# Scores of gated linear attention as half-width products copied under masks, one product for selected keys and values, and compressed values padded to 128 rows

## The chip, the cores and the metric

The kernel runs on one core of a Trainium2 chip. The metric is the device time of one execution in microseconds (us), the median of the runs. The core's engines work beside each other and wait for one another through semaphores: TensorE (PE: products and transposes; PEld is its loading of the stationary operand), VectorE (DVE), ScalarE (ACT), GpSimd (POOL) and SyncE (SP, which only starts the transfers here).

## The reference

One decoder layer over 256 positions of width 2048. One projection of the normalised input feeds two mixers: four heads of gated linear attention (GLA) and eight query heads of sparse attention (NSA) with two key and value heads. Their outputs go through one output projection, and a gated feed-forward layer follows. All of it is in float32. Cut to the parts that the change touches:

```python
def gla_mixer(q, k, v, gate_lr, out_gate, gate_w2, gate_b, norm_g):
    ...
    qc = chunks(q.astype(jnp.float32) * GLA_DK ** -0.5, GLA_DK)
    ...
    def step(state, inp):
        qi, ki, vi, gi = inp
        b = jnp.cumsum(gi, axis=2)
        o_inter = jnp.einsum('bhtd,bhde->bhte', qi * jnp.exp(b), state)
        decay = jnp.exp(jnp.where(causal, b[:, :, :, None, :] - b[:, :, None, :, :], -jnp.inf))
        scores = jnp.einsum('bhtd,bhsd,bhtsd->bhts', qi, ki, decay)
        o_intra = jnp.einsum('bhts,bhse->bhte', scores, vi)
        ...
    o = rms_norm(o, norm_g) * jax.nn.silu(out_gate.astype(jnp.float32)).reshape(b_, s, h, GLA_DV)

def nsa_mixer(...):
    ...
    v_cmp = compress(heads(vc_raw, hk), v_pos, v_w1, v_w2)      # 15 compressed blocks
    ...
        sc = jnp.einsum('bhgqd,bhnd->bhgqn', qb, k_cmp).astype(jnp.float32) * scale
        mc = cmp_end[None, :] <= t[:, None]
        pc = jax.nn.softmax(jnp.where(mc, sc, NEG), axis=-1) * mc
        o_cmp = jnp.einsum('bhgqn,bhnd->bhgqd', pc.astype(v_cmp.dtype), v_cmp)
    ...
```

## The kernel before

**Stages.** The input projection runs over column groups of `w_in`, 512 wide, in the order that the last lines of the kernel give (L1062 to L1068): first the low-rank gate with half of the output gate, then the other half, then q, k and v of GLA, then the raw keys and values of NSA (`C_KC` compressed, `C_KS` selected, `C_KW` window), then its queries. The output projection follows in two halves (`w_out_half`), and then the feed-forward layer, which takes most of the program. Each weight is loaded in float32 and split into two parts (`split`, L129 on ScalarE and L130 on VectorE), and every product of a float32 matrix is made as three products of the parts (`chunk`, L261: high by high, high by low, low by high). Such a product of 512 columns is one instruction. Products that aren't split (the scores of GLA, L513) are plain float32, which TensorE runs as two passes, so each of them shows up twice in the trace.

**Work beside the projections.** Everything small is written as generators that are put on two lists, `urgent` and `later`. `drive` takes one step of them for every few steps of a projection. A scheduler then fixes the order on each engine; engines take their own list in order. So the mixers run between the products of the projections, and the engines' lists decide who waits for whom.

**GLA.** Inside a chunk the decay between two positions is built from levels: `LEVELS` is 0 (the diagonal) and the block lengths 1 to 64. `gla_decay` makes, per pair of heads, one array `e[l]` per level, in which every second block of length l holds decayed queries and the others decayed keys (L484 to L495). `gla_scores` is run for 4 heads and 2 blocks of 128 positions, 8 times in all. For each level it multiplies `e[l]` with itself (L513), 128 by 128, four levels to a bank of PSUM; L515 multiplies the four with their masks `lmask` into a scratch array `m`, and after both banks L518 adds the eight levels up. The masks hold ISQ (the scale of the queries) where a level counts and 0 elsewhere. `gla_out` (L525 to L535) multiplies the scores with the values, `gla_turn` turns the result for the output projection.

**NSA.** `ev_kv(0)` empties the banks of the selected keys and values, `ev_kv(1)` those of the window's. `compress` makes 15 compressed keys and values for each head; the values lie in `vcm`, 15 rows. `nsa_scores` computes the probabilities, `c` being those of the 15 compressed blocks; `nsa_out` turns them (L193, through `turn`) and multiplies them with the values (L817), first with `vcm`.

**Buffers.** PSUM has eight banks of 128 by 512 (`bank()`), which projections and side work share. SBUF slots come from rings: `g4` (24), `g2` (13), `g1` (7), `small` (12).

The lines that decide how often L261 runs for selected keys and values, where `parts` gives each column group its own bank:

```python
for i, (a, m) in enumerate(((xh, wh), (xh, wl), (xl, wh))):
    for (off, w), bk in zip(parts, banks):
        last["mm"] = mm(bk[t], a[:, k, t * P:(t + 1) * P], m[:, off:off + w], ...)
...
proj(C_KS, ev_kv(0), ((0, 256), (256, 256)))
```

Of the kernel before, what the change touches and what calls it, by code (L numbers as in the profile page):

```python
# [9 lines left out]
F32R = mybir.dt.float32r  # L10
# [26 lines left out]
def kernel(  # L37
# [37 lines left out]
    def f32(t):  # L75
        return t.bitcast(F32)
# [131 lines left out]
    def cols_rest():  # L208
        for _ in range(8):
            yield  # L210
        with behind(last["dma"]):
            small_loads()
        for _ in range(20):
            yield
        pc = bank()
        transpose(pc[:, 0:P], rows2)
        transpose(pc[:, P:P + 20], rows[:20, :], 20)
        nc.vector.tensor_copy(cols[:, 36:164], pc[:, 0:P])
        nc.vector.tensor_copy(cols[:, 16:36], pc[:, P:P + 20])
        TS(kgain, gains[:, 1:4], gains[:, 0:1], None, ALU.mult)  # L220

# [128 lines left out]
    def constants():  # L350

        nc.gpsimd.memset(lmask, ISQ)
        for li, l in enumerate(LEVELS):
            if l == 0:
                affine(lmask[:, li, :], [[-1, P]], 0, 1)
                affine(lmask[:, li, :], [[1, P]], 0, -1)
                continue
            nb = P // (2 * l)
            v = lmask[:, li, :].rearrange("p (b h i) -> p b h i", h=2, i=l)
            nc.gpsimd.memset(v[:, :, 0, :], 0.0)  # L360
            affine(v[:, :, 1, :], [[-2 * l, nb], [0, l]], 0, 1)
            affine(v[:, :, 1, :], [[2 * l, nb], [0, l]], l - 1, -1)

        cnegf = g1([2, P])
        nc.gpsimd.memset(cnegf, 0.0)
        affine(cnegf, [[0, 2], [-1, P]], 0, 1, NEG)
        nc.vector.tensor_copy(cneg, cnegf)
        nc.vector.tensor_copy(identb, ident)

        nc.gpsimd.memset(mneg, 0.0)  # L370
        affine(mneg, [[P, NT], [-16, NCMP]], -31, 1, NEG)
        nc.gpsimd.memset(mone, 1.0)
        affine(mone, [[P, NT], [-16, NCMP]], -31, 1, 0.0)
# [131 lines left out]
    def gla_scores(h, b, res):  # L505
        tb = slice(b * P, (b + 1) * P)
        m, e = g4([NLEV, P]), dec[h // 2]
        for half in range(2):
            p = bank()
            for j in range(4):  # L510
                l = LEVELS[4 * half + j]
                u, w = (e[l][:, h % 2, tb],) * 2 if l else (kT[:, h, tb], qT[:, h, tb])
                mm(p[:, j * P:(j + 1) * P], u, w, start=True, stop=True)  # L513
                yield
            TT(m[:, 4 * half:4 * half + 4, :], p.rearrange("p (l t) -> p l t", l=4),  # L515
               lmask[:, 4 * half:4 * half + 4, :], ALU.mult)
        sc = g1([P])
        nc.vector.tensor_reduce(sc, m.rearrange("p l t -> p t l"), AX.X, ALU.add)  # L518
        res["s"] = sc

    def gla_out(h, r0, r1):
# [6 lines left out]
        act(sof, pof[:, 0:P], AF.Copy, scale=ISQ)  # L528
# [13 lines left out]
        TS(ro, ss, 1.0 / 256, EPS, ALU.mult, ALU.add)  # L542
# [61 lines left out]
    def ev_kv(br):  # L604
        def f(banks):
# [5 lines left out]
            for t in range(NT):  # L611
                pv = banks[1][t][:, :S]
# [42 lines left out]
    vcm = [cp.tile([NCMP, 2, P], F32R, name=f"vcm{i}") for i in range(2)]  # L655
    N2 = 2 * NCMP

    def compress():

        uT = st["uT"]  # L660
        for w, w1 in enumerate((k_w1, v_w1)):
# [44 lines left out]
            else:  # L706
                for h in range(2):
                    mm(pk[:NCMP, h * P:(h + 1) * P], hid[:, h * NCMP:(h + 1) * NCMP], cw2[:, 1, :], start=True, stop=True)
                in_parts(vcm[0], vcm[1], pk[:NCMP, :S].rearrange("p (h d) -> p h d", h=2))
# [35 lines left out]
    def nsa_scores(kv, t, res):  # L745
# [25 lines left out]
        c = small([4, NCMP])  # L771
# [18 lines left out]
        res.update(pr=pr, c=c)  # L790

    def nsa_out(kv, t, res):
# [6 lines left out]
        def turn(i):  # L799
            pt = bank()  # L800
            n = P if i else NCMP
            for j in range(4):
                src = pr[j][:, todo[i][0], todo[i][1] * P:(todo[i][1] + 1) * P] if i else c[:, j, :]
                transpose(pt[:n, j * P:(j + 1) * P], src)
                if j % 2:
                    yield
            pts.append((g2([512], F32R)[:n], g2([512], F32R)[:n]))
            in_parts(*pts[i], pt[:n, :])
# [256 lines left out]
    drive([proj(C_KC, ev_kc), proj(C_KS, ev_kv(0), ((0, 256), (256, 256))),  # L1065
# [45 lines left out]
```

## Time and profile before

| what | value |
|---|---|
| time, median of 3 runs | 1139.52 us (1139.39 to 1140.56) |
| span of the profiled execution | 1138.1 us, that is 1.4 us under the median of the runs |
| TensorE busy | 1125.4 us, 99% of the span |
| VectorE busy | 926.0 us, 81% |
| ScalarE busy | 604.7 us, 53% |
| GpSimd busy | 23.5 us, 2% |
| granted TensorE clock | 1.00 throughout |
| transfers | 213.44 MB, 188 GB/s on average |

How to read it: a page shows one profiled execution. The groups give line, engine, operation, output and input with their shapes, the number of instructions, busy time and the mean duration of one in ns, and behind the bar how long the engine had been idle just before them and what ended that. Matmuls are pipelined: an instruction lasts longer than the distance to the next one, so TensorE's pace is read from the distance between starts, or from the length of a stretch divided by the number of its products. A span of the chain or of the timeline begins with its start in us and its length in us.

### The profile page before, as it was taken

The numbers are of one execution on the slowest core, as the hardware profiler recorded it, in microseconds if no ns is written. First come the engines' busy times: TensorE is split into PE (matmuls) and PEld (weight loads), VectorE is DVE, ScalarE is ACT, GpSimd is POOL, SyncE is SP. The second block draws the span as 40 slices with busy tenths as digits, with TensorE's granted clock in tenths as the row PEclk, the third lists the DMA queues.
The fourth block names the chain that finished last, engine by engine and source line by source line (L and its number), as shares of the span: only waits on it lengthen the run. The fifth ranks groups of instructions, "written<-read, shape, count | busy, mean of one in ns | idle before, by whom it ended". The sixth has DMA issues, their size and how long they took to land.

```text
span 1138.1 us, 14334 instructions
## 1 busy us (share of the span) xinstructions
PE 1125.4 (99%) x5545; PEld 932.0 (82%) x5545; DVE 926.0 (81%) x1150; ACT 604.7 (53%) x742; POOL 23.5 (2%) x53
## 2 busy tenths in 40 slices
PE   9999999999999999999999999999999999999998
PEld 8888889998777787788888888888888888888886
DVE  6547779987479578999898897979798897979793
ACT  7654466544476486564555555364555455454540
POOL 3000000100000000000000000000000000000000
PEclk9999999999999999999999999999999999999999
DMA  7655543445843354665666566565665665665652
GB/s 273 226 185 185 185 148 113 154 149 165 301 163 112 116 180 150 209 235 192 213 196 198 200 201 204 185 213 191 198 211 187 204 202 186 196 225 172 219 186 74
DMA packets 110446, 213.44 MB, mean 188 GB/s; under 512 B 5110, under 2 KB 8218, under 8 KB 110379
## 3 DMA queue, kind: packets, MB, share of 16 engines
q1 hardware_dynamic: 110378, 212.54, 56.5%
q8 instruction: 43, 0.70, 0.2%
q14 instruction: 25, 0.20, 0.0%
HBM read 210.42 MB, written 2.10 MB: 187 GB/s over the span
## 4 chain that ended last, share of the span: by engine, by line
PE 93%; DVE 3%; DMA 1%; issue 1%; ACT 0%; POOL 0%; SPq 0%; DVEq 0%
PE bank L261 48%; PE bank L964 39%; PE bank L193 3%; PE bank L817 1%; PE bank L759 1%; DMA raw<-in_w_out_dram 1%; DVE lo L130 1%; DMA g<-in_x_dram 1%; PE bank L513 1%; DVE g L515 0%; DVE g L518 0%; DVE g L490 0%; DVE ftwo L565 0%; PE bank L675 0%; DVE g L489 0%
## 5 line engine op out<-in xcount | busy, mean ns | idle before, releaser
L964 PE MATMUL bank<-ftwo,g 128*128 128x512 f32 x1935 | 451.2, 392 | 1.1 <-DVE ftwo L565 0.8
L964 PEld LDWEIGHTS bank<-ftwo,g 128*128 128x128 f32 x1935 | 359.8, 188 | 75.7 <-DVE ftwo L565 1.6
L564 ACT ACTIVATE ftwo<-fraw 128x1536 fp32r<-128x1536 f32 (+1 forms) x130 | 230.8, 1775 | 202.2 <-PE bank L964 78.1
L565 DVE TENSOR_TENSOR ftwo<-fraw,ftwo 128x1536 fp32r<-128x1536 f32 (+1 forms) x130 | 273.4, 2110 | 66.5 <-ACT ftwo L564 66.5
L261 PE MATMUL bank<-hi,g 128*128 128x512 f32 (+3 forms) x1152 | 326.3, 366 | 1.2 <-ACT hi L129 0.6
L261 PE MATMUL bank<-ftwo,g 128*128 128x512 f32 x1056 | 241.6, 389 | 0.0
L261 PEld LDWEIGHTS bank<-ftwo,g 128*128 128x128 f32 x1056 | 198.1, 188 | 41.1
L261 PEld LDWEIGHTS bank<-hi,g 128*128 128x128 f32 x1152 | 199.3, 189 | 31.2 <-issue 2.3
L130 DVE TENSOR_TENSOR lo<-raw,hi 128x1024 fp32r<-128x1024 f32 (+3 forms) x125 | 151.4, 1217 | 75.0 <-ACT hi L129 74.4
L261 PE MATMUL bank<-lo,g 128*128 128x512 f32 (+1 forms) x576 | 195.3, 365 | 0.5 <-DVE lo L130 0.5
L129 ACT ACTIVATE hi<-raw 128x1024 fp32r<-128x1024 f32 (+3 forms) x125 | 131.3, 1056 | 110.1 <-PE bank L261 77.6
L564 ACT ACTIVATE ftwo<-g 128x1024 fp32r<-128x1024 f32 x86 | 89.1, 1057 | 97.0 <-DVE g L983 66.6
L261 PEld LDWEIGHTS bank<-lo,g 128*128 128x128 f32 x576 | 102.6, 189 | 15.3 <-DVE lo L130 1.0
L565 DVE TENSOR_TENSOR ftwo<-g,ftwo 128x1024 fp32r<-128x1024 f32 x86 | 103.2, 1217 | 0.0
L1055 DVE TENSOR_TENSOR g<-bank,g 128x512 f32<-128x512 f32 (+1 forms) x96 | 59.9, 643 | 16.3 <-PE bank L261 15.2
L983 DVE TENSOR_TENSOR g<-fraw 128x1024 f32<-128x1024 f32 x43 | 52.4, 1218 | 0.9 <-DMA fraw<-in_w_up_dram 0.9
L564 ACT ACTIVATE g<-bank 128x512 fp32r<-128x512 f32 (+1 forms) x50 | 29.4, 592 | 39.6 <-PE bank L193 30.9
L193 PE MATMUL bank<-ident,g 128*128 128x128 f32 (+2 forms) x214 | 37.9, 275 | 3.4 <-DMA g<-in_x_dram 1.5
L565 DVE TENSOR_TENSOR g<-bank,g 128x512 fp32r<-128x512 f32 (+1 forms) x50 | 33.6, 680 | 6.1 <-ACT g L564 6.1
L193 PEld LDWEIGHTS bank<-ident,g 128*128 128x128 f32 (+2 forms) x214 | 27.1, 140 | 13.4 <-issue 2.3
L984 DVE TENSOR_TENSOR g<-g,fraw 128x512 f32<-128x512 f32 x43 | 29.6, 687 | 0.7
L985 DVE TENSOR_TENSOR g<-g,fraw 128x512 f32<-128x512 f32 x43 | 29.6, 688 | 0.7
(192 smaller groups left out, 635.8 us busy)
## 6 DMA issues: line engine op xcount, KB each, us to landing
fraw<-in_w_down_dram SPq DMA_DIRECT2D x44, 1024.0 KB, 5.0
fraw<-in_w_gate_dram SPq DMA_DIRECT2D x86, 512.0 KB, 3.8
fraw<-in_w_up_dram SPq DMA_DIRECT2D x86, 512.0 KB, 4.7
raw<-in_w_in_dram SPq DMA_DIRECT2D x36, 1024.0 KB, 5.1
raw<-in_w_out_dram SPq DMA_DIRECT2D x16, 1024.0 KB, 5.2
raw<-in_w_in_dram SPq DMA_DIRECT2D x4, 1072.0 KB
g<-in_x_dram SPq DMA_DIRECT2D x7, 512.0 KB, 10.0
raw<-in_w_in_dram SPq DMA_DIRECT2D x3, 1056.0 KB, 11.2
```

What stands on the lines that cost most here:

```text
L129: act(h[:, i:i + n], r[:, k + i:k + i + n], AF.Copy)
L130: TT(o[:, i:i + n], r[:, k + i:k + i + n], f32(h[:, i:i + n]), ALU.subtract)
L193: return nc.tensor.transpose(o, i, ident[:n, :n])
L261: last["mm"] = mm(bk[t], a[:, k, t * P:(t + 1) * P], m[:, off:off + w], start=(first_ and k == 0 and i == 0), stop=(end and k == 3 and i = ...
L513: mm(p[:, j * P:(j + 1) * P], u, w, start=True, stop=True)
L564: act(hi, ps, AF.Copy)
L565: TT(lo, ps, f32(hi), ALU.subtract)
L964: mm(banks[q], x, m, start=new and i == 0, stop=todo[q] == 0)
L983: TT(s1, r[:, 1:3], r[:, 3:4].to_broadcast([P, 2, 512]), ALU.add)
L984: TT(s2[:, 0], s1[:, 1], r[:, 1], ALU.add)
L985: TT(s2[:, 1], s2[:, 0], r[:, 0], ALU.add)
L1055: TT(h_sb[n][:, t, cs], banks[i][t][:, cs], h_sb[n][:, t, cs], ALU.add)
```

## The change

Four edits, of which the first is the largest.

1. In `gla_scores` each level but the diagonal is multiplied only with the blocks that hold queries: 64 of the 128 columns. The products of a level lie side by side in the bank. Instead of the multiplication with the masks, the scratch array and the sum, the score array `sc` is filled with zeros by GpSimd, and each level is copied into its place by a copy that writes only where the mask isn't zero (`copy_predicated`, VectorE). The levels 8 to 64 come first now. The masks hold 1, and the scale ISQ moves into the norm behind (`gng`, and the constant in `ro`).
2. The selected keys and values are projected as one product of 512 columns into one bank for each block of positions, where there were two of 256 columns into two banks.
3. The compressed values `vcm` and the probabilities `c` are padded with zeros to 128 rows or columns, so that L817's products with `vcm` take 128 rows. `c` moves from a slot of `small` to one of `g2`.
4. VectorE gets one more instruction early on, the scaling of `gng`.

```diff
@@ -218,6 +218,7 @@
         nc.vector.tensor_copy(cols[:, 36:164], pc[:, 0:P])
         nc.vector.tensor_copy(cols[:, 16:36], pc[:, P:P + 20])
         TS(kgain, gains[:, 1:4], gains[:, 0:1], None, ALU.mult)
+        TS(gng, gng, ISQ, None, ALU.mult)
 
 
     def flip(src, q, gcol, hi, lo):
@@ -349,7 +350,7 @@
 
     def constants():
 
-        nc.gpsimd.memset(lmask, ISQ)
+        nc.gpsimd.memset(lmask, 1.0)
         for li, l in enumerate(LEVELS):
             if l == 0:
                 affine(lmask[:, li, :], [[-1, P]], 0, 1)
@@ -504,18 +505,26 @@
 
     def gla_scores(h, b, res):
         tb = slice(b * P, (b + 1) * P)
-        m, e = g4([NLEV, P]), dec[h // 2]
-        for half in range(2):
-            p = bank()
-            for j in range(4):
-                l = LEVELS[4 * half + j]
-                u, w = (e[l][:, h % 2, tb],) * 2 if l else (kT[:, h, tb], qT[:, h, tb])
-                mm(p[:, j * P:(j + 1) * P], u, w, start=True, stop=True)
+        e, sc = dec[h // 2], g1([P])
+        nc.gpsimd.memset(sc, 0.0)
+        for part in (LEVELS[4:], LEVELS[:4]):
+            p, at = bank(), 0
+            todo = []
+            for l in part:
+                if l == 0:
+                    u, w, o, n = kT[:, h, tb], qT[:, h, tb], p[:, at:at + P], P
+                    todo.append((sc, lmask[:, 0, :], o))
+                else:
+                    u = e[l][:, h % 2, tb]
+                    w, so, mk = (a.rearrange("p (n r i) -> p n r i", r=2, i=l)[:, :, 1, :]
+                                 for a in (u, sc, lmask[:, LEVELS.index(l), :]))
+                    o, n = p[:, at:at + P // 2].rearrange("p (n i) -> p n i", i=l), P // 2
+                    todo.append((so, mk, o))
+                mm(o, u, w, start=True, stop=True)
+                at += n
                 yield
-            TT(m[:, 4 * half:4 * half + 4, :], p.rearrange("p (l t) -> p l t", l=4),
-               lmask[:, 4 * half:4 * half + 4, :], ALU.mult)
-        sc = g1([P])
-        nc.vector.tensor_reduce(sc, m.rearrange("p l t -> p t l"), AX.X, ALU.add)
+            for t in todo:
+                nc.vector.copy_predicated(t[0], t[1].bitcast(mybir.dt.uint32), t[2])
         res["s"] = sc
 
     def gla_out(h, r0, r1):
@@ -525,7 +534,7 @@
         mm(pof[:, 0:P], off[:, 0:P], off[:, P:], start=True, stop=True)
         yield
         sof = g1([P])
-        act(sof, pof[:, 0:P], AF.Copy, scale=ISQ)
+        act(sof, pof[:, 0:P], AF.Copy)
         ve = slice(h * 256, (h + 1) * 256)
         po = bank()
         mm(po[:, 0:256], r0["s"], v_sb[0][:, ve], start=True, stop=True)
@@ -539,7 +548,7 @@
             junk = g1([256])
             act(junk, po[:, t * 256:(t + 1) * 256], AF.Square, accum_out=ss[:, t:t + 1])
         ro = small([NT])
-        TS(ro, ss, 1.0 / 256, EPS, ALU.mult, ALU.add)
+        TS(ro, ss, ISQ * ISQ / 256, EPS, ALU.mult, ALU.add)
         rsqrt_(ro, ro)
         y = g2([NT, 256])
         gv = slice((h % 2) * 256, (h % 2 + 1) * 256)
@@ -609,7 +618,7 @@
             if br == 1:
                 gate = st["gate"] = cp.tile([P, NT, 24], F32, name="gate")
             for t in range(NT):
-                pv = banks[1][t][:, :S]
+                pv = banks[0][t][:, S:] if br == 0 else banks[1][t][:, :S]
                 vh = st["vh"][:, br, t, :]
                 act(vh, pv, AF.Copy, scale=rx[:, t:t + 1])
                 STT(st["vl"][:, br, t, :], pv, rx[:, t:t + 1], f32(vh), ALU.mult, ALU.subtract)
@@ -652,12 +661,14 @@
         STT(kl, pv, g, f32(kh), ALU.mult, ALU.subtract)
 
     kcm = cp.tile([P, 2 * NCMP], F32, name="kcm")
-    vcm = [cp.tile([NCMP, 2, P], F32R, name=f"vcm{i}") for i in range(2)]
+    vcm = [cp.tile([P, 2, P], F32R, name=f"vcm{i}") for i in range(2)]
     N2 = 2 * NCMP
 
     def compress():
 
         uT = st["uT"]
+        for t in vcm:
+            nc.gpsimd.memset(f32(t), 0.0)
         for w, w1 in enumerate((k_w1, v_w1)):
             ph = bank()
             nc.vector.memset(ph[:, :P], 0.0)
@@ -706,7 +717,7 @@
             else:
                 for h in range(2):
                     mm(pk[:NCMP, h * P:(h + 1) * P], hid[:, h * NCMP:(h + 1) * NCMP], cw2[:, 1, :], start=True, stop=True)
-                in_parts(vcm[0], vcm[1], pk[:NCMP, :S].rearrange("p (h d) -> p h d", h=2))
+                in_parts(vcm[0][:NCMP], vcm[1][:NCMP], pk[:NCMP, :S].rearrange("p (h d) -> p h d", h=2))
             yield
 
     nq, sc = {}, {}
@@ -768,7 +779,9 @@
                 act(pr[j][:, b, :], sv[:, b, :], AF.Exp, bias=nb[:, j, b:b + 1], scale=scv[:, j:j + 1],
                     accum_out=sums[:, j, b:b + 1])
 
-        c = small([4, NCMP])
+        cpad = g2([4, P])
+        nc.gpsimd.memset(cpad, 0.0)
+        c = cpad[:, :, :NCMP]
         TT(c, pc_[:, :4 * NCMP].rearrange("p (h n) -> p h n", h=4), scv.unsqueeze(2).to_broadcast([P, 4, NCMP]), ALU.mult)
         TT(c, c, mneg[:, t, :].unsqueeze(1).to_broadcast([P, 4, NCMP]), ALU.add)
         mx = small([4])
@@ -787,7 +800,7 @@
         for j in range(4):
             for b in range(2):
                 TS(pr[j][:, b, :], pr[j][:, b, :], rs[:, j, b:b + 1], None, ALU.mult)
-        res.update(pr=pr, c=c)
+        res.update(pr=pr, c=cpad)
 
     def nsa_out(kv, t, res):
         pr, c, tb = res["pr"], res["c"], slice(t * P, (t + 1) * P)
@@ -798,14 +811,13 @@
 
         def turn(i):
             pt = bank()
-            n = P if i else NCMP
             for j in range(4):
                 src = pr[j][:, todo[i][0], todo[i][1] * P:(todo[i][1] + 1) * P] if i else c[:, j, :]
-                transpose(pt[:n, j * P:(j + 1) * P], src)
+                transpose(pt[:, j * P:(j + 1) * P], src)
                 if j % 2:
                     yield
-            pts.append((g2([512], F32R)[:n], g2([512], F32R)[:n]))
-            in_parts(*pts[i], pt[:n, :])
+            pts.append((g2([512], F32R), g2([512], F32R)))
+            in_parts(*pts[i], pt)
 
         po = bank()
         yield from turn(0)
@@ -1062,7 +1074,7 @@
     drive([proj(C_GO + 512, ev_go(1)), proj(0, ev_conv(0, to_qk(qT))), proj(512, ev_conv(4, to_qk(kT))),
            proj(1024, ev_conv(8, to_v(0))), proj(1536, ev_conv(12, to_v(1)))], 1.5)
     later.append(gla_mix())
-    drive([proj(C_KC, ev_kc), proj(C_KS, ev_kv(0), ((0, 256), (256, 256))),
+    drive([proj(C_KC, ev_kc), proj(C_KS, ev_kv(0)),
            proj(C_KW, ev_kv(1), ((0, 256), (256, 280))), proj(C_NQ, ev_nq(0))], 2.5)
     later.append(nsa_mix())
     drive([proj(C_NQ + 512, ev_nq(1))], 2.5)
```

How the order on the engines changes, at three places. **TensorE, where the selected keys and values are projected and the second score unit is computed.** Before (L513 are the scores, `g_...` their level array; L261 is the projection, `bank_1628` and `bank_1630` are the two banks of one block of positions):

```order
L513 MATMUL bank_1695<-g_237_1572 128x128
L261 MATMUL bank_1629<-hi_1638,g_24_144 128x256
L261 MATMUL bank_1631<-hi_1638,g_24_144 128x256
L513 MATMUL bank_1721<-g_16_129,g_17_130 128x128
L261 MATMUL bank_1629<-lo_1639,g_24_144 128x256
L261 MATMUL bank_1631<-lo_1639,g_24_144 128x256
L513 MATMUL bank_1721<-g_221_1481 128x128
```

and the same place of the changed kernel (L523 are the scores, L262 the projection):

```order
L523 MATMUL bank_1623<-g_237_1573 128x64
L262 MATMUL bank_1636<-lo_1644,g_24_144 128x512
L523 MATMUL bank_1686<-g_16_129,g_17_130 128x128
L262 MATMUL bank_1636<-hi_1643,g_25_145 128x512
L523 MATMUL bank_1686<-g_221_1482 128x64
L262 MATMUL bank_1635<-hi_1643,g_24_144 128x512
L523 MATMUL bank_1686<-g_227_1503 128x64
```

Each pair of projections of 256 columns is one of 512, into two banks in all instead of four, and the scores have 64 columns, but for the diagonal. Behind the C_KW projection the list of TensorE is the same as before but for these shapes, the order of the levels and the paddings; over the program it has 96 products fewer.

**VectorE, where the first score units are put together.** Before:

```order
L502 TENSOR_TENSOR g_238_1584<-g_238_1584,g_16_129 128x2x128
L515 TENSOR_TENSOR g_239_1590<-bank_1602,lmask 128x512
L490 TENSOR_TENSOR g_77_554<-g_77_554 128x256
L518 TENSOR_REDUCE g_242_1613<-g_239_1590 128x128
L494 COPY g_245_1619<-g_17_130 128x256
L495 TENSOR_TENSOR g_245_1619<-g_245_1619,g_16_129 128x256
L515 TENSOR_TENSOR g_243_1615<-bank_1616,lmask 128x512
```

and now (L527 is the copy under a mask; `g_239_1591` and `g_242_1621` are the score arrays of two units):

```order
L503 TENSOR_TENSOR g_238_1585<-g_238_1585,g_16_129 128x2x128
L527 COPY_PREDICATED g_239_1591<-lmask,bank_1593 128x8x8
L495 COPY g_244_1626<-g_17_130 128x256
L527 COPY_PREDICATED g_239_1591<-lmask,bank_1593 128x4x16
L496 TENSOR_TENSOR g_244_1626<-g_244_1626,g_16_129 128x256
L527 COPY_PREDICATED g_239_1591<-lmask,bank_1593 128x2x32
L527 COPY_PREDICATED g_242_1621<-lmask,bank_1623 128x8x8
L527 COPY_PREDICATED g_239_1591<-lmask,bank_1593 128x64
```

Eight short copies stand for two wide multiplications and a sum, and those of two units alternate.

**VectorE, in the first projection**, where the scaling of `gng` comes to stand between a weight split (L130) and the turned input (L239, before L238):

```order
L239 SCALAR_TENSOR_TENSOR g_45_276<-bank_288,cols,g_44_275 128x256 x2
L130 TENSOR_TENSOR lo_302<-raw_277,hi_301 128x2x528
L221 TENSOR_SCALAR gng<-gng 128x256
L239 SCALAR_TENSOR_TENSOR g_56_358<-bank_361,cols,g_55_357 128x256 x2
L130 TENSOR_TENSOR lo_374<-raw_359,hi_373 128x2x528
```

It waits there for the load of `gng`, and L239 behind it waits with it.

## The prediction

> **What bounds the kernel now.** I read the page first, then the windows of the stage that the change touches, then TensorE's waits.
>
> ```profile
> PE 1125.4 (99%) x5545; PEld 932.0 (82%) x5545; DVE 926.0 (81%) x1150; ACT 604.7 (53%) x742; POOL 23.5 (2%) x53
> PE 93%; DVE 3%; DMA 1%; issue 1%; ACT 0%; POOL 0%; SPq 0%; DVEq 0%
> 538.94 36.04 PE bank L964 x159
> 17.96 5.92 PE bank L261 x48
> ```
>
> TensorE is busy 99% of the span, and 93% of the chain of work that ended last lies on it: the kernel is worth what TensorE's list is worth, and only fewer or shorter products, or fewer waits of TensorE, move the time. The last two rows, from that chain, give its pace: a product of 512 columns takes 36.04/159 = 0.227 us, and one of 256 or 272 in turn 5.92/48 = 0.123 us, so 0.117 to 0.120 at 256. The 3% on VectorE are one stage:
>
> ```profile
> core 0: us, PE busy (x) PEld busy (x) DVE busy (x) ACT busy (x) POOL busy (x), PEclk, DMA share, GB/s
> 160.00:180.00 20.00, 20.00 (x116) 17.36 (x115) 19.04 (x43) 18.82 (x34) 0.00 (x0) 1.00 0.39 117
> 180.00:200.00 20.00, 18.97 (x155) 18.42 (x155) 19.80 (x31) 9.15 (x18) 1.24 (x1) 1.00 0.30 100
> 200.00:220.00 20.00, 18.15 (x144) 17.34 (x143) 19.18 (x37) 10.54 (x25) 1.06 (x2) 1.00 0.40 126
> ```
>
> From 160 to 220 us, where the selected keys and values are projected beside the first five of the eight score units, VectorE is busy 58.0 of 60 us, and TensorE is idle 2.9. TensorE's own waits name what was late:
>
> ```profile
> PE bank L193 <- DVE g L548: 1.2, 1, 1.2
> PE bank L261 <- DVE g L615: 0.6, 1, 0.6
> PE bank L513 <- DVE g L515: 0.5, 1, 0.5
> PE bank L261 <- DVE lo L130: 0.5, 1, 0.5
> 200.33 0.27 PE L513 MATMUL bank<-g 128*128 128x128 f32 x1
> 201.75 0.30 PE L193 MATMUL bank<-ident,g 128*128 128x128 f32 x1 [1.15 <-DVE g L548]
> ```
>
> All four are VectorE with too much ahead of it. They show 2.8 us, but cost more: an instruction is drawn 0.27 us long and the next could follow after 0.11, so the wait of the last two rows (starts 1.42 apart) costs 1.3, not 1.15. With some 0.2 for each of the four, and half a microsecond of delays too short to show as idle, this stage holds about 4.2 us of waits.
>
> **1. Scores with 64 columns: nothing on TensorE.** The instructions are as many as before, with half the columns. Whether that shortens them is read from a float32 product with still fewer columns, L762's with 15:
>
> ```profile
> 175.25 0.38 PE L513 MATMUL bank<-g,g 128*128 128x128 f32 x2
> 175.39 0.47 PE L261 MATMUL bank<-hi,g 128*128 128x512 f32 x1
> 175.71 0.38 PE L513 MATMUL bank<-g 128*128 128x128 f32 x2
> ...
> 327.77 0.29 PE L762 MATMUL bank<-kcm,g 128*128 128x15 f32 x2
> 327.92 0.48 PE L261 MATMUL bank<-hi,g 128*128 128x512 f32 x1
> 328.23 0.38 PE L193 MATMUL bank<-ident,sm 128*15 128x128 f32 x2
> ```
>
> From the start of the pair of passes to the start of what follows the projection product: 0.46 us with 128 columns, 0.46 with 15. Take off 0.227 for the 512 columns, and a pass takes 0.115 to 0.117 either way. What fills it is the load of the stationary operand, 128 columns in both:
>
> ```profile
> L513 PEld LDWEIGHTS bank<-g 128*128 128x128 f32 x112 | 18.0, 189 | 1.1 <-DVE g L495 0.3
> L762 PEld LDWEIGHTS bank<-kcm,g 128*128 128x128 f32 x32 | 5.2, 195 | 0.2
> L193 PEld LDWEIGHTS bank<-ident,sm 128*15 128x15 f32 x16 | 1.5, 96 | 0.9
> ```
>
> It lasts 189 and 195 ns for the same 128 columns and 96 for 15, and the change keeps `e[l]` whole as the stationary operand. So 56 products of 64 columns save 0; at L762's pace, up to 0.01 us more for each, they cost 0.5. I take +0.3; the gainful bound, if columns alone counted, is 56 x 2 x 0.056 = -6.3. The Trainium skill would take that bound: "TensorE: Matmul & The Clock Gate", Back-to-back issue gap, gives about 60 cycles for up to 64 columns and 134 for 128, and names the weight load as a second limit for streams; L762's rows decide for the second limit.
>
> **2. VectorE's part of the scores.** The multiplications and the sum that go, and the nearest rows for the copies that come:
>
> ```profile
> L515 DVE TENSOR_TENSOR g<-bank,lmask 128x512 f32<-128x512 f32 x16 | 10.9, 685 | 1.1 <-PE bank L513 1.0
> L518 DVE TENSOR_REDUCE g<-g 128x128 f32<-128x1024 f32 x8 | 15.9, 1990 | 0.1
> L772 DVE TENSOR_TENSOR sm<-bank,sc 128x60 f32<-128x60 f32 x4 | 0.8, 205 | 0.0
> L639 DVE TENSOR_SCALAR g<-bank,sm 128x128 f32<-128x128 f32 x8 | 2.4, 344 | 0.0
> ```
>
> A unit loses 2 x 0.685 + 1.99 = 3.36 us. No row shows a copy under a mask. It reads PSUM and SBUF and has 64 columns (7 of them) or 128 (one); 0.205 (60 columns, two operands, one in PSUM) bounds it from below, 0.344 (128 columns from PSUM) from above. I take 0.22 and 0.29, near the former: 7 x 0.22 + 0.29 = 1.83 us for a unit, 2.75 at the upper end. Eight units free 12.2 us of VectorE (4.9 at least), the five of the full stage 7.6 (3.0 at least). Each copy follows another one into the same array, which is the reason for a value above the lowest row.
>
> VectorE off the path is worth nothing; in this stage it is what TensorE waits for. Each of the four waits lies behind at least one unit's sum and two multiplications, 3.36 us that become 1.8, and is itself at most 1.3 long. Edit 3 below helps two of them. What is late next: the turned output of the first head (L548, now L557) still hangs on ScalarE's squares and GpSimd's power, so I leave 0.9 us in the stage and take **-3.3** of the 4.2. Bounds: 0 and -4.2.
>
> **3. One product of 512 columns for selected keys and values.** 16 row blocks x 2 position blocks x 3 parts = 96 pairs of 0.234 to 0.240 us become 96 products of 0.227: 0.7 to 1.2 us less, I take **-0.9**. The projection then holds two banks of PSUM instead of four while the scores run, which is what L513 and L261 waited for behind L515 and L615.
>
> **4. Padding to 128 rows.** L817's products with 15 rows stand between products with 128:
>
> ```profile
> 330.97 0.40 PE L261 MATMUL bank<-hi,g 128*128 128x512 f32 x1
> 331.30 0.50 PE L817 MATMUL bank<-g,vcm 15*128 15x512 f32 x1
> 331.73 0.66 PE L193 MATMUL bank<-ident,g 128*128 128x128 f32 x4
> ...
> 332.55 0.73 PE L817 MATMUL bank<-g,vcm 15*128 15x512 f32 x2
> 333.20 0.50 PE L261 MATMUL bank<-lo,g 128*128 128x512 f32 x1
> L817 PE MATMUL bank<-g,vcm 15*128 15x512 f32 x12 | 4.9, 461 | 0.0
> ```
>
> Compare ends, since the pace stands there. L261 ends at 331.37 and the 15 rows at 331.80: 0.43 where 0.227 is the pace, so 0.20 is lost going in. The four turns behind end at 332.39, 0.59 later where four take 0.436 (0.109 each): 0.15 lost coming out; behind the pair (333.28 to 333.70) 0.20. The 12 products come in eight such runs (one and two for each of four tiles), so 8 x (0.15 to 0.20 + 0.20) = 2.8 to 3.2 us; I take **-3.0**. This part of the span is TensorE's own, nothing else is late there. With 128 rows all products have one shape and the loss should go whole. The Trainium skill is of two minds: "TensorEngine Tiling (Array Packing)", Key Properties, says that changing the tiling mode drains the engine, which agrees with the 0.20; "TensorE: Matmul & The Clock Gate", Step-by-step, says that the row count doesn't matter to the weight load, by which padding would save 0. The turns and copies of 128 instead of 15 rows take as long as before, since length goes by columns.
>
> **5. The rest.** GpSimd gets 14 fillings with zeros of 128 to 512 columns, each under the 0.96 us that 1024 columns take in the last row below, on an engine busy 23.5 us; the first copies of a unit come after its products, long behind its filling. ScalarE and the order of the transfers keep their work. The scaling of `gng` waits for a load in front of L238:
>
> ```profile
> 25.23 0.87 DVE L238 SCALAR_TENSOR_TENSOR g<-bank,cols,g 128x256 fp32r<-128x256 f32 x2 [2.61 <-ACT g L236]
> 22.86 0.36 SPq L155 DMA_DIRECT2D gng<-in_gla_norm_g_dram  x1
> w2b<-in_gla_gate_w_dram SPq DMA_DIRECT2D x1, 32.0 KB, 1.8
> g<-in_gla_conv_w_dram SPq DMA_DIRECT2D x1, 32.0 KB, 6.7
> L380 POOL MEMSET g<- 128x1024 f32 x1 | 1.0, 962 | 0.0
> ```
>
> VectorE was idle until 25.23. The load starts at 22.86; if it takes 1.8 us as its neighbour did, nothing is late, and if 6.7, L238 is 4.4 late. A quarter of this projection has 48 products, about 5.9 us; the third starts at 24.8, and L238 serves the fourth, from 30.7. So I cost it at 0, and at 2 us if the load takes the longer time.
>
> **The sum.** +0.3 - 3.3 - 0.9 - 3.0 = -6.9 us against the span of 1138.1, which lies 1.4 under the median of the runs: 1139.5 - 6.9 = **1132.6**. What a measurement of this kernel can tell from no change is about 0.2%, 2.3 us.
>
> **The rivals.**
>
> - *The stage's waits stay* (17%): the scheduler has set a new order, and TensorE may wait elsewhere for VectorE, at the copies or at the turned output. For it: TensorE takes its list in order, and the levels 8 to 64, made last, are now wanted first. Against it: VectorE is freed by 3.0 us even at the upper price. -0.9 - 3.0 + 0.3 = -3.6: 1135.9.
> - *Columns count* (8%): the scores' passes halve. -6.3 in place of +0.3: 1126.0. L762 speaks against it. It is what the issue gap of the Trainium skill's "TensorE: Matmul & The Clock Gate" alone would give.
> - *Padding saves nothing* (5%): the loss at L817 belongs to something else, such as its waits. -6.9 + 3.0 = -3.9: 1135.6. The same 0.20 at the runs shown speaks against it.
> - *Copies under a mask are slow* (4%): 40 of them stand in the stage where VectorE has 2.0 us left and loses 5 x 3.36 = 16.8. At L515's 0.685 us each they take 27.4, TensorE waits 8.6 us more, and with -3.6 for the rest the time is 1144.5. It decides from (16.8 + 2.0 + 3.6)/40 = 0.56 us for a copy, above every row of its size.
> - *Much of all this fails at once* (4%): within 2 us of before.
>
> **How the numbers follow.** The forecast keeps 62%, with 1130.9 to 1134.5 for its own (waits left 0 to 2.2, the scores' 0 to 0.5, the bounds of 3 and 4). The range reaches up to the second and fourth case and leaves out the third and the last two, 16%: 1130.0 to 1137.0. Faster by over 0.2% are the forecast and most of the first three rivals: 0.88; within it, a part of the first rival and most of the last: 0.07; slower: 0.05.
>
> **What would show it.** Scores: L523's passes of 64 columns still 0.11 us apart, the weight loads at 189 ns. VectorE: under 54 us busy between 160 and 220, copies near 0.22 us. TensorE's waits on VectorE there under 1 us in all. Selected keys and values: 96 instructions fewer. L829's products with `vcm` at the length of the others, nothing lost before or behind. I would be wrong if the copies last over 0.5 us, if the turned output is still waited for, or if the passes come closer together.

## The result and the profile after

| | before | after |
|---|---|---|
| time, median of 4 runs each | 1140.04 us (1139.39 to 1141.26) | 1131.12 us (1130.67 to 1134.38) |
| ratio | | 0.9926, 95% interval 0.9912 to 0.9941 |
| span of the profiled execution | 1138.1 us | 1129.5 us (its own time 1131.56) |

The change makes the kernel 8.9 us faster by the medians and 8.6 us by the two profiled spans; the forecast was 6.9. The page of the changed kernel, busy times and the chain that ended last:

```profile
PE 1121.2 (99%) x5449; PEld 928.5 (82%) x5449; DVE 914.2 (81%) x1191; ACT 604.4 (54%) x742; POOL 29.3 (3%) x67
PE 96%; DMA 2%; DVE 1%; ACT 0%; issue 0%; SPq 0%; POOL 0%; DVEq 0%; ACTq 0%
```

TensorE has 96 instructions fewer, VectorE's share of the chain has fallen from 3% to 1%. Where the time went is read from four places that both programs pass in the same order: the gate's first product, the compression's first, the first product with compressed values, the feed-forward's first. Timeline rows of before (the third place is in the prediction, L817 at 331.30), then of after; the first column is the start in us:

```profile
43.19 0.69 PE L394 MATMUL bank<-lrT,w2b 17*128 17x256 f32 x2
280.47 0.75 PE L675 MATMUL bank<-raw,g 128*30 128x128 f32 x20
430.28 0.39 PE L964 MATMUL bank<-hi,g 128*128 128x512 f32 x1
```

```profile
43.75 0.69 PE L395 MATMUL bank<-lrT,w2b 17*128 17x256 f32 x2
275.80 0.75 PE L686 MATMUL bank<-raw,g 128*30 128x128 f32 x20
326.08 0.39 PE L829 MATMUL bank<-g,vcm 128*128 128x512 f32 x1
422.18 0.39 PE L976 MATMUL bank<-hi,g 128*128 128x512 f32 x1
```

| stretch | before | after | difference | forecast |
|---|---|---|---|---|
| start to the gate | 43.19 | 43.75 | +0.56 | 0 |
| gate to compression (projections and scores) | 237.28 | 232.05 | -5.23 | -3.9 |
| compression to the first compressed values | 50.83 | 50.28 | -0.55 | 0 |
| compressed values to the feed-forward | 98.98 | 96.10 | -2.88 | -3.0 |

From the feed-forward to the span's end it is 707.8 and 707.3 us. The first and third differences are no more than what executions differ by: over the kernels below the first stretch varies by 0.9 us, and the third lies between 49.7 and 50.9 in all of them but e6b_copies_thrice. So nearly all of the gain lies in the two stretches that the prediction named, and the first of them gave 1.3 us more than forecast. The windows of this stage, of the changed kernel (columns as in the prediction):

```profile
160.00:180.00 20.00, 20.00 (x106) 16.92 (x105) 19.04 (x43) 18.50 (x33) 0.00 (x0) 1.00 0.49 159
180.00:200.00 20.00, 20.00 (x116) 17.26 (x114) 16.82 (x57) 10.77 (x23) 1.97 (x3) 1.00 0.24 70
200.00:220.00 20.00, 20.00 (x137) 18.59 (x136) 18.00 (x47) 10.83 (x27) 2.35 (x2) 1.00 0.51 167
```

VectorE is busy 53.9 instead of 58.0 of 60 us, and TensorE's 2.9 idle us are gone. None of TensorE's four waits is left in this stage. Its largest wait on VectorE's `lo` is now 0.37 us long and stands behind the stage, at 301.73 us:

```profile
PE bank L262 <- DVE lo L130: 0.4, 1, 0.4
```

The new groups, and a few rows of TensorE's timeline with scores of 128 and of 64 columns:

```profile
L523 PEld LDWEIGHTS bank<-g 128*128 128x128 f32 x112 | 18.9, 190 | 1.8
L527 DVE COPY_PREDICATED g<-lmask,bank 128x64 f32<-128x64 uint32 x56 | 13.1, 244 | 1.8 <-PE bank L523 1.2
L527 DVE COPY_PREDICATED g<-lmask,bank 128x128 f32<-128x128 uint32 x8 | 2.4, 298 | 0.4
L829 PE MATMUL bank<-g,vcm 128*128 128x512 f32 x12 | 4.2, 403 | 0.0
```

```profile
182.81 0.38 PE L523 MATMUL bank<-g,g 128*128 128x128 f32 x2
182.95 0.48 PE L262 MATMUL bank<-hi,g 128*128 128x512 f32 x1
183.27 0.33 PE L523 MATMUL bank<-g 128*128 128x64 f32 x2
183.41 0.48 PE L262 MATMUL bank<-hi,g 128*128 128x512 f32 x1
183.72 0.33 PE L523 MATMUL bank<-g 128*128 128x64 f32 x2
```

A pair of passes and the product behind it take 0.46 us with 128 columns (182.81 to 183.27) and 0.45 with 64 (183.27 to 183.72). The copies last 0.244 and 0.298 us, 13.1 + 2.4 = 15.5 us for eight units.

### The profile page after: what moved, and what is told of

Its sections match the earlier page's. It is cut to its first block, busy times and chain, and to the rows that moved or that the text cites. A ratio compares the mean times of both kernels' runs of the same rounds, so it can differ in the third digit from the quotient of the medians.

```text
span 1129.5 us, 14206 instructions
## 1 busy us (share of the span) xinstructions
PE 1121.2 (99%) x5449; PEld 928.5 (82%) x5449; DVE 914.2 (81%) x1191; ACT 604.4 (54%) x742; POOL 29.3 (3%) x67
## 4 chain that ended last, share of the span: by engine, by line
PE 96%; DMA 2%; DVE 1%; ACT 0%; issue 0%; SPq 0%; POOL 0%; DVEq 0%; ACTq 0%
PE bank L262 49%; PE bank L976 39%; PE bank L193 3%; DMA raw<-in_w_out_dram 1%; PE bank L523 1%; PE bank L829 1%; PE bank L770 1%; DMA g<-in_x_dram 1%; DVE lo L130 0%; DVE ftwo L574 0%; ACT hi L129 0%; PE bank L686 0%; PE bank L395 0%; PE bank L773 0%; PE bank L772 0%
## 5 line engine op out<-in xcount | busy, mean ns | idle before, releaser
L262 PE MATMUL bank<-hi,g 128*128 128x512 f32 (+1 forms) x1088 | 323.3, 376 | 0.0
L262 PE MATMUL bank<-ftwo,g 128*128 128x512 f32 x1056 | 241.6, 389 | 0.0
L262 PEld LDWEIGHTS bank<-ftwo,g 128*128 128x128 f32 x1056 | 198.1, 188 | 41.1
L262 PEld LDWEIGHTS bank<-hi,g 128*128 128x128 f32 x1088 | 192.3, 188 | 30.4 <-issue 1.7
L130 DVE TENSOR_TENSOR lo<-raw,hi 128x1024 fp32r<-128x1024 f32 (+3 forms) x125 | 152.2, 1224 | 75.6 <-ACT hi L129 75.0
L262 PE MATMUL bank<-lo,g 128*128 128x512 f32 (+3 forms) x544 | 194.7, 376 | 0.4 <-DVE lo L130 0.4
L262 PEld LDWEIGHTS bank<-lo,g 128*128 128x128 f32 x544 | 98.7, 189 | 15.5 <-DVE lo L130 0.8
L573 ACT ACTIVATE g<-bank 128x512 fp32r<-128x512 f32 x50 | 29.6, 600 | 38.0 <-PE bank L193 29.1
L193 PE MATMUL bank<-ident,g 128*128 128x128 f32 (+2 forms) x230 | 41.0, 276 | 1.4 <-ACT g L907 0.7
L193 PEld LDWEIGHTS bank<-ident,g 128*128 128x128 f32 (+2 forms) x230 | 30.0, 141 | 12.2 <-ACT g L907 1.9
L574 DVE TENSOR_TENSOR g<-bank,g 128x512 fp32r<-128x512 f32 x50 | 33.7, 683 | 4.6 <-ACT g L573 4.5
```

Of the source, the lines that this page charges most:

```text
L130: TT(o[:, i:i + n], r[:, k + i:k + i + n], f32(h[:, i:i + n]), ALU.subtract)
L193: return nc.tensor.transpose(o, i, ident[:n, :n])
L573: act(hi, ps, AF.Copy)
L574: TT(lo, ps, f32(hi), ALU.subtract)
```

## The experiments

Two theories stood against each other for the stage of the scores: VectorE's time ended TensorE's waits, or something else that the change brings did (two banks of PSUM set free, fewer columns, the new order of the products). For the compressed values it was the shape of the products against the waits around them. Besides the median, each row gives two stretches of the profiled execution as above. In some executions the granted clock dips between 40 and 60 us (last section), so the first stretch is given a second time from the 150th product behind the gate's last, at about 80 us, which is past that place; the products up to there have one order in all kernels. The ratios of the kernels from e1 on are to the kernel before as it was timed beside them, with medians of 1140.34 (e1 to e4), 1140.70 (e5, e6, e6b, e8) and 1140.96 (e7, e9, e10).

| kernel | median, us | ratio to before, 95% | gate to compression | the same from about 80 us | compressed values to feed-forward |
|---|---|---|---|---|---|
| before | 1140.04 | 1 | 237.28 | 200.19 | 98.98 |
| after | 1131.12 | 0.9926 (0.9912 to 0.9941) | 232.05 | 194.96 | 96.10 |
| e1_pad_only | 1135.80 | 0.9962 (0.9949 to 0.9974) | 237.19 | 200.10 | 96.13 |
| e2_kv_only | 1139.70 | 0.9996 (0.9987 to 1.0004) | 237.28 | 200.19 | 98.99 |
| e3_scores_only | 1135.26 | 0.9958 (0.9945 to 0.9970) | 232.98 | 195.89 | 99.05 |
| e4_no_pad | 1135.17 | 0.9954 (0.9941 to 0.9968) | 232.09 | 195.00 | 99.00 |
| e5_128_columns | 1131.43 | 0.9916 (0.9901 to 0.9932) | 233.85 | 195.18 | 96.10 |
| e6_copies_twice | 1140.39 | 0.9994 (0.9984 to 1.0004) | 241.51 | 202.83 | 96.10 |
| e6b_copies_thrice | 1149.70 | 1.0076 (1.0057 to 1.0096) | 243.51 | 204.83 | 95.51 |
| e8_gate_pad | 1130.30 | 0.9906 (0.9892 to 0.9921) | 230.94 | 194.96 | 96.13 |
| e9_levels_turned | 1139.93 | 0.9995 (0.9986 to 1.0004) | 237.09 | 200.01 | 99.02 |
| e10_short_sum | 1136.85 | 0.9970 (0.9959 to 0.9981) | 237.00 | 196.76 | 99.00 |
| e7_pad_64 | 1135.66 | 0.9959 (0.9945 to 0.9974) | 233.67 | 195.00 | 99.00 |
| e7_pad_96 | 1131.84 | 0.9922 (0.9905 to 0.9938) | 233.62 | 194.96 | 96.13 |

### The parts one by one

**e1_pad_only** is the kernel before with the padding alone:

```
-    vcm = [cp.tile([NCMP, 2, P], F32R, name=f"vcm{i}") for i in range(2)]
+    vcm = [cp.tile([P, 2, P], F32R, name=f"vcm{i}") for i in range(2)]
...
-        c = small([4, NCMP])
+        cpad = g2([4, P])
+        nc.gpsimd.memset(cpad, 0.0)
+        c = cpad[:, :, :NCMP]
```

> The kernel before with the padding to 128 rows alone. Theory (products with 15 rows cost 0.20 us going in and 0.15 to 0.20 coming out, eight runs of them): 2.9 us less than before, about 1137.1; the 12 products with vcm as long as their neighbours, about 400 ns instead of 461. Rival (the time lost there belongs to the waits around it, padding moves nothing): within 0.5 us of before.

The last stretch falls from 98.98 to 96.13 us, by 2.85, and nothing moves in the stage of the scores. The 12 products last 404 ns. The median is 4.5 us lower with 3.0 to 5.8 in its interval. The profiled spans differ by 3.4 us (1138.1 and 1134.7), and 2.85 of that stand in this stretch; the remainder is spread over the others and isn't settled. The padding stands by itself.

**e2_kv_only** has the one product of 512 columns alone, **e3_scores_only** the scores with their copies alone, **e4_no_pad** both. The edit of e2 (that of e3 is the first of the change):

```
-                pv = banks[1][t][:, :S]
+                pv = banks[0][t][:, S:] if br == 0 else banks[1][t][:, :S]
...
-    drive([proj(C_KC, ev_kc), proj(C_KS, ev_kv(0), ((0, 256), (256, 256))),
+    drive([proj(C_KC, ev_kc), proj(C_KS, ev_kv(0)),
```

> The kernel before with the selected keys and values in one product of 512 columns, nothing else. Theory (VectorE is what TensorE waits for in the stage of the scores; the product only saves the shorter pairs): 0.8 to 1.2 us less than before, and about 3 to 4 us of TensorE's delays left from 160 to 220 us. Rival (TensorE waited for PSUM banks, and two banks freed are what ended the waits): 4 to 5 us less than before, and the delays gone.

> The kernel before with the scores' 64 columns and copies under a mask alone (with the scaling that moves to gng and to the norm's factor). Theory (VectorE's relief ends the waits): 3.3 to 4.2 us less than before, VectorE under 55 us busy from 160 to 220 us. Rival (banks): less than 1.5 us saved, TensorE still waits for banks at L261 and at the scores.

> The changed kernel without the padding: scores and the one product for selected keys and values. By the two traces of before and after this should carry 5.2 us plus up to 0.5: 5.2 to 5.8 us less than before, 2.9 more than the changed kernel. Theory (waits of one cause, ended by VectorE's relief): e2 and e3 together save about as much as this, 0.9 + 3.3 to 4.2. Rival (both parts end the same waits, either would do): e2 and e3 together save clearly more than this, by 2 us or more.

e2 is a miss for the times of both theories: the stretch stays at 237.28 us, though its 96 instructions are gone. Its waits of TensorE on VectorE in this stage:

```profile
PE bank L261 <- DVE lo L130: 2.3, 3, 1.6
PE bank L193 <- DVE g L548: 1.0, 1, 1.0
PE bank L513 <- DVE g L495: 0.5, 1, 0.5
```

That is 3.8 us where before showed 2.8, as the first theory said of the delays: TensorE comes earlier and waits longer for the same VectorE. The two banks did not help either; of the four old waits, the two behind L515 and L615 are gone, and others stand for them. e3 takes 4.30 us out of the stretch, VectorE being busy 53.4 us from 160 to 220, with no wait on VectorE left there; e4 takes out 5.19, and its two main stretches together are 2.9 us longer than those of the changed kernel, as expected. So the product of 512 columns is worth 0.0 alone and 5.19 - 4.30 = 0.89 us behind the relief of VectorE. The parts don't end the same wait twice, as the rival of e4 had it, nor do they simply add, as its theory had it (0.0 + 4.30 against 5.19); one makes the other count.

### What ended the waits

**e9_levels_turned** makes the second half of the levels first, as the changed kernel does, and **e10_short_sum** shortens the sum, both in the kernel before:

```
-        for half in range(2):
+        for half in (1, 0):
```

```
-        nc.vector.tensor_reduce(sc, m.rearrange("p l t -> p t l"), AX.X, ALU.add)
+        nc.vector.tensor_reduce(sc, m[:, 0:2, :].rearrange("p l t -> p t l"), AX.X, ALU.add)
```

> The kernel before with the two halves of the levels in the changed kernel's order (8 to 64 first), all multiplications and sums kept. Theory (VectorE's time is what ended the waits): VectorE as busy as before, the stretch from the gate's products to the compression's stays at 237.3 us or within 1 us of it. Rival (the new order of the products ended the waits): it falls by 3 us or more, toward the 232.98 of the scores alone.

> The kernel before with the sum over two levels instead of eight (the other six are left out of the sum; every product and multiplication is still made). VectorE's sum reads 256 instead of 1024 columns and should take about 0.6 instead of 1.99 us, as much relief as the copies bring (3.36 to 1.83 us for a unit), with the products as they were. Theory (VectorE's time): the stretch from the gate's products to the compression's falls from 237.3 to between 233 and 234.5 us. Rival (order, banks or fewer columns): within 1 us of 237.3.

The new order moves the stretch by 0.2 us. The short sum leaves six of the eight levels out, so its scores are not the layer's; with products of 128 columns, four banks and nearly the old order, it takes 200.19 to 196.76, by 3.43 us (the 237.00 of the whole stretch holds 3.0 us of a dipped clock). What it changes is one group of VectorE, and one wait on VectorE is left in the stage:

```profile
L518 DVE TENSOR_REDUCE g<-g 128x128 f32<-128x256 f32 x8 | 3.4, 422 | 0.1
PE bank L261 <- DVE g L547: 0.5, 1, 0.5
```

422 instead of 1990 ns frees 1.57 us in a unit, and that alone brings 80% of what the scores as changed bring (3.43 of 4.30). So less time on VectorE is enough to end most of the waits, without the new order, fewer banks or fewer columns. It doesn't bring the last 0.87 us, although the copies free less (3.36 - 1.94 = 1.42 us in a unit). The wait that is left, 0.54 us at 216.78 us, is for L547, the product with the norm's factor, which had itself waited 0.81 us for GpSimd's power: it is of the kind for which the prediction left 0.9 us. Of the other 0.3, e5 below puts 0.22 on the columns. What ends that last wait in e3 isn't shown.

**e5_128_columns** is the changed kernel with full score products:

```
-                    w, so, mk = (a.rearrange("p (n r i) -> p n r i", r=2, i=l)[:, :, 1, :]
-                                 for a in (u, sc, lmask[:, LEVELS.index(l), :]))
-                    o, n = p[:, at:at + P // 2].rearrange("p (n i) -> p n i", i=l), P // 2
-                    todo.append((so, mk, o))
+                    w, o, n = u, p[:, at:at + P], P
+                    todo.append(tuple(a.rearrange("p (n r i) -> p n r i", r=2, i=l)[:, :, 1, :]
+                                      for a in (sc, lmask[:, LEVELS.index(l), :], o)))
```

> The changed kernel with all 128 columns in each score product; the copies still take only the 64 that are wanted, now strided out of the bank. Theory (the load of the stationary operand sets a pass, and columns cost nothing here): within 0.5 us of the changed kernel, the stretch from the gate's products to the compression's (232.05 us in the changed kernel) between 231.9 and 232.6, copies under 0.3 us. Rival (columns count): 56 x 2 x 0.056 = 6.3 us more, about 1137.4.

From 80 us on it takes 195.18 against 194.96: doubling the columns of 56 products costs 0.22 us, not 6.3, and the copies last as before (245 and 299 ns). The whole stretch, 233.85, looks outside the theory's bounds; the windows show why:

```profile
40.00:60.00 20.00, 20.00 (x78) 15.08 (x77) 8.46 (x11) 11.96 (x12) 0.00 (x0) 0.91 0.48 159
```

The mean granted clock was 0.91 there, long before the first score. In the Trainium skill ("TensorE: Matmul & The Clock Gate", Back-to-back issue gap) the table by columns has under half the cycles for up to 64 columns, but as the gap of an isolated product; in a stream of weight loads and products, the section says, both set the spacing. This pair of kernels agrees with the latter: where each float32 pass brings its own stationary operand of 128 columns, half the columns change almost nothing.

**e6_copies_twice** and **e6b_copies_thrice** put work on VectorE in the changed kernel:

```
-            for t in todo:
+            for t in todo + todo:
```

> The changed kernel with each copy under a mask made twice, with the same result: VectorE gets some 1.4 us (by the spacing of copies in a row, 1.49 us for nine) to 1.9 us (by their mean durations) more for a unit, 7 to 9.7 us in the five units of the full stage, where it has 6.1 of 60 us left. Theory (the stage is lost and won by VectorE's time): TensorE's waits come back, the stretch from the gate's products to the compression's is 1 to 4 us longer than 232.05. Rival (the new order of products ended the waits, not VectorE's time): within 0.5 us of 232.05.

> The changed kernel with each copy under a mask made three times: 14 to 19 us more on VectorE in the full stage. Theory: the part beyond the 6.1 us left is TensorE's wait, 8 to 13 us more than the changed kernel, and every further copy costs its own time on VectorE. Rival (order): within 0.5 us.

e6 came out dearer than its theory, 202.83 - 194.96 = 7.9 us in the stretch against 1 to 4. e6b is 18.6 us longer in the median and 17.9 in the profiled span, against 8 to 13; but in the stretch it is 204.83 - 194.96 = 9.9 us, as its theory had it. Of the rest, 1.6 us are the clock between 40 and 60 us, and 7.4 stand in the next stretch, from the compression to the first compressed values (57.7 instead of 50.3 us), where TensorE waits for a weight's `hi` from ScalarE and the mean clock is 0.66 from 316 to 326 us:

```profile
PE bank L262 <- ACT hi L129: 3.7, 1, 3.7
```

In e6 the loss isn't plain load, since VectorE is not full: it is busy 16.27 and 17.08 us in the two windows from 180 to 220. Rows of e6's timeline, VectorE then TensorE:

```profile
195.18 0.22 DVE L527 COPY_PREDICATED g<-lmask,bank 128x64 f32<-128x64 uint32 x1
198.21 0.17 DVE L551 TENSOR_SCALAR sm<-sm 128x2 f32<-128x2 f32 x1 [2.81 <-ACT g L549]
198.29 1.22 DVE L130 TENSOR_TENSOR lo<-raw,hi 128x1024 fp32r<-128x1024 f32 x1
```

```profile
196.71 0.59 PE L544 MATMUL bank<-g,g 128*128 128x256 f32 x2
199.56 0.50 PE L262 MATMUL bank<-lo,g 128*128 128x512 f32 x1 [2.26 <-DVE lo L130]
```

VectorE stands 2.81 us at the norm's factor (L551), which waits for ScalarE's squares of what TensorE has just made at L544; `lo` for the projection is queued behind it, and TensorE waits 2.26 us for `lo`. In the changed kernel L551 and `lo` follow each other in the same way; there VectorE waits 0.83 us and TensorE not at all. So the largest wait comes from an operation at the head of VectorE's list, not from overload, and why the squares come so much later in e6 stays open. Two more waits follow, 0.89 us for a copy (L527) at 217.81 and 1.10 us for `lo` at 220.16. The mean clock from 200 to 220 is 0.91, which cost 1.6 us between 40 and 60 us; by that estimate some 2 of the 7.9 us are left without a cause. So these two runs show that the stage can be lost on VectorE again; they don't measure what a copy costs.

### How many rows, and a version with more of it

**e7_pad_64** and **e7_pad_96** pad the compressed block's products to fewer rows; with n = 64 or 96, and as many rows of `vcm`:

```
-                transpose(pt[:, j * P:(j + 1) * P], src)
+                transpose(pt[:n, j * P:(j + 1) * P], src)
...
-            pts.append((g2([512], F32R), g2([512], F32R)))
-            in_parts(*pts[i], pt)
+            pts.append((g2([512], F32R)[:n], g2([512], F32R)[:n]))
+            in_parts(*pts[i], pt[:n, :])
```

> The changed kernel with the compressed block's products padded to 64 rows instead of 128. Theory A (every product of other than the full array's rows costs 0.2 us going in and out): the stretch from the first of these products to the feed-forward is 99.0 us, as in the kernel before, against 96.1 with 128 rows. Rival B (the loss goes by the missing rows): 97.7. Rival C (only small counts of rows cost): 96.1.

> The changed kernel with the compressed block's products padded to 96 rows. Theory A1 (any number of rows under 128 costs the 0.2 us): 99.0 us in that stretch. Theory A2 (what costs is a change of the array's division, and 96 rows need the whole array): 96.1. Rival B (by the missing rows): 96.9.

The group of these products in e7_pad_64, then in e7_pad_96:

```profile
L830 PE MATMUL bank<-g,vcm 64*128 64x512 f32 x12 | 4.9, 460 | 0.0
```

```profile
L830 PE MATMUL bank<-g,vcm 96*128 96x512 f32 x12 | 4.2, 404 | 0.0
```

64 rows cost exactly what 15 cost, 99.00 us in the stretch; 96 rows cost nothing, 96.13. The loss is no matter of the rows' count but of a border between 64 and 96. The Trainium skill fits that: in "TensorEngine Tiling (Array Packing)", Available Configurations, rows come in tiles of 32, 64 or 128, so that 15 and 64 fit a smaller tile and 96 don't, and its Key Properties name a drain at every change of mode. That these products run in such a tile, and that the loss is a drain, no row shows; the border is measured.

**e8_gate_pad** pads another place with few rows, the gate's products of 17, in the changed kernel:

```
-    w2b = cp.tile([17, 512], F32, name="w2b")
+    w2b = cp.tile([P, 512], F32, name="w2b")
+    nc.gpsimd.memset(w2b, 0.0)
...
-    lrT = cp.tile([17, S], F32, name="lrT")
+    lrT = cp.tile([P, S], F32, name="lrT")
```

> The changed kernel with the gate's operands w2b and lrT padded from 17 to 128 rows in the same way (zeros in w2b), a version meant to beat both kernels. Theory (every run of products with few rows costs about 0.2 us going in and about 0.2 coming out): the three runs of L395 end 0.15 to 0.18 us late and the products behind them 0.20 to 0.21, 1.1 us in all, and it goes: the time from the first of L395's runs to the product behind the last falls by 1.0 to 1.2 us. Rival (those ends are late because the products read float32 or 256 columns): nothing changes.

TensorE's timeline of e8, from the first of the gate's runs to the product behind the last:

```profile
43.05 0.59 PE L396 MATMUL bank<-lrT,w2b 128*128 128x256 f32 x2
...
44.37 1.03 PE L396 MATMUL bank<-lrT,w2b 128*128 128x256 f32 x4
45.05 0.58 PE L263 MATMUL bank<-hi,g 128*128 128x512 f32 x1
```

It ends at 45.63, 2.58 us after the start; in the changed kernel the same takes 43.75 to 47.42, 3.67 us. The loss of 1.09 us goes, as worked out. The median is the lowest of all, 1130.30 us; 0.8 under that of the changed kernel, which was timed in another set of runs, so the trace and not the medians carries this gain.

## Why the prediction was right, and where it was off

**Bound.** TensorE's list and VectorE's share in one stage: as read. Nearly all of the gain came from the two stretches named, and nothing new of size is waited for.

**Scores with 64 columns, +0.3.** Right in that the columns don't set the pass (pairs 0.45 and 0.46 us apart): e5 puts them at 0.22 us in all, on the gaining side, so the +0.3 had the wrong sign. That it is the load that fills the pass (still 190 ns) fits, but no run shortens it for a score product. The prediction's third row, 96 ns for a load of 15 columns, shows no shorter pass: before the change two such turns start at 328.23 and 328.34 us, 0.11 apart like turns whose load has 128 columns, so there the 128 moving columns may be what fills it.

**VectorE's relief, -3.3 of 4.2.** Right in mechanism (e10, e9), with the term too small: e3 takes out 4.30 us, about 4.1 without the 0.22 of the columns, so practically all the waits ended. The 0.9 us that I left for the turned output behind ScalarE's squares and GpSimd's power is not there; no wait at it appears after. In e10, which only shortens the sum, 0.54 us of that kind stayed. The copies were near the estimate, 0.244 and 0.298 us for 0.22 and 0.29, a unit 15.5/8 = 1.94 for 1.83.

**One product of 512 columns, -0.9.** The size is right, 0.89 us, but not as a term of its own. The prediction added it beside the waits and let it help two of them by its banks; e2 shows 0.0 alone and no help. While the stage waited for VectorE, shorter products of TensorE only lengthened the wait. The term held in the sum because the relief came with it, not for the reason given.

**Padding, -3.0.** -2.88 in the pair of traces and -2.85 alone: 0.36 us for each of the eight runs, against 0.35 to 0.40.

**The rest, 0.** TensorE never waited for GpSimd's 14 fillings. VectorE did wait 2.9 us for the load of `gng`, from about 23 to 26 us, and no wait of TensorE on VectorE appears behind it. But the end of the program is 0.5 us shorter, which the prediction doesn't have: from the start of TensorE's last product to the span's end it is 5.0 us in the four kernels that keep GpSimd's old list (before, e2, e9, e10) and 4.55 to 4.57 in the ten with new fillings. Why stays open.

**The rivals.** The stage's waits stay: they went in e3. Columns count: refuted by e5. Padding saves nothing: refuted by e1. Slow copies: a copy takes 0.244 or 0.298 us, about half of the 0.56 from which it would decide.

The difference to the forecast, 8.6 - 6.9 = 1.7 us by spans, is thus 1.3 in the stage (1.0 on the waits, 0.3 charged to the scores) and 0.5 at the end, less 0.1 of the padding; the start (+0.56) and the stretch from the compression to the first compressed values (-0.55) cancel.

## What to carry to other kernels

Price a saving on the engine that waits only after the relief of the engine that it waits for: in a stage bound by VectorE, 96 instructions fewer on TensorE gave 0.0 us alone and 0.89 behind the relief. Look through the list of products for the few with a row count of 64 or less between full ones, and pad them with zeros over the border, where each run of them costs 0.36 us. Halving the columns of 56 products that each bring their own stationary operand gained 0.22 us; what paid was VectorE's shorter work on them, one copy of 64 columns each instead of a multiplication and a sum, and e5 has that with full products too.

## What was not expected of the hardware

- Programs that are alike up to 80 us ran there at different clocks. From the gate's last product to the 150th behind it took 34.23 us in seven of the profiles and 35.81 in five of them, where the mean clock from 40 to 60 us was 0.91 (77 or 78 products in the window where the changed kernel had 85), and 37.26 in one with 0.83. Inside the window it is a halving: in slices of 1 us the clock of e5 is 0.50 for about 3.4 us, and that of e10 for about twice as long, although TensorE is drawn busy throughout. What starts it no run shows. That is 1.6 to 3.0 us, as much as an edit of this change, and a reason to compare stretches beside medians. The medians carry it as well: of the 15 runs of the kernel before timed beside e1 to e4, the seven with a mean clock of 0.998 took 1140.34 to 1142.05 us, the eight others 1139.34 to 1140.65. Three slices of e5:

```profile
46.00:47.00 1.00, 1.00 (x5) 0.74 (x5) 0.70 (x1) 0.98 (x3) 0.00 (x0) 0.93 1.05 406
48.00:49.00 1.00, 1.00 (x3) 0.77 (x3) 0.00 (x0) 0.99 (x2) 0.00 (x0) 0.50 0.00 0
51.00:52.00 1.00, 1.00 (x6) 0.83 (x5) 0.16 (x1) 0.98 (x2) 0.00 (x0) 1.00 0.00 0
```

- Copies under a mask overlap: nine in a row took 1.49 us, 0.166 each, though one lasts 244 ns.

```profile
183.04 1.49 DVE L527 COPY_PREDICATED g<-lmask,bank 128x64 f32<-128x64 uint32 x9
```
